# Decoder layer on one core: a quarter of the compression's page loads on GpSimd's queue, the loads' rooms in another order, two rings exchanged

## The chip, the cores and the metric

The kernel runs on one core of a Trainium2 chip. The metric is the device time of one execution in microseconds, as a median of runs. Engines are named as in the profile: PE (TensorE matmuls; PEld its weight loads), DVE (VectorE), ACT (ScalarE), POOL (GpSimd), SP (SyncE, which here only issues DMAs). A queue is the in-order list of instructions of one engine; what it issues as DMA moves later, on the 16 DMA engines.

## The reference

One decoder layer on 320 tokens (256 of a prompt, 64 of eight samples), width 2048: a first SwiGLU block with LayerNorm, a mixer (retention heads and sparse attention with a paged cache of 2048 past positions per sample), a second SwiGLU block. The change touches one part of the mixer, the compression of the cached keys and values of the eight samples:

```python
def compress(x, pos_emb, w1, w2):
    ...
    chunks = x[:, :n_chunks * CMP_STRIDE].astype(F32).reshape(B, n_chunks, CMP_STRIDE, NSA_KV_HEADS, NSA_HD)
    ...
    h = jnp.einsum('pd,pdf->f', pos_emb.astype(F32), w1f)
    for r in range(R):
        h = h + jnp.einsum('bnskd,sdf->bnkf', chunks, w1r[r])[:, r:r + n_cmp]
    return jnp.einsum('bnkf,fd->bnkd', jax.nn.gelu(h), w2.astype(F32))
```

It runs once on keys and once on values, over all pages of the cache that the page table names (8 samples x 16 pages of 128 positions).

## The kernel before, in words

All large products are made of three matmuls with a high and a low part of each factor (`mm3`, lines 211 to 216); `split` (lines 218 to 220) makes the two parts of a tile, the high one on ACT (L219), the low one on DVE (L220). One stream of emitted instructions sets the order on every engine; background tasks are woven in by a clock of estimates. [...]

The stage of interest, `compress` (L708 on), stands between the first SwiGLU block and the projection `w_in_nsa`. In the trace it runs from 946.9 us to 1279.0 us.

- **Work.** Eight pairs of samples (pairs 0 to 3 are keys, 4 to 7 values) of 16 steps n each, 128 steps in all. A step is 18 matmuls of 256 columns. m counts steps by twos (0 to 63). The data of a pair comes in two halves, 16 halves in all, each for four values of m.
- **Loads.** A half is 32 pages' tiles of 128 rows x 128 values, 64 KB each, one DMA per tile, since each page's address is read from the page table. `cx_load` calls `pages` for four tiles at a time; `pages` loads four addresses into registers of SP (L597) and issues four DMAs on SP's queue (L601). So SP issues 32 DMAs per half.
- **Rooms.** A half lies in one of three rooms of 16 KB per partition: `x0` and `x1`, cut from two rings which otherwise hold the layer's input parts, and `raw`, the weight buffers. The table `ROOMS` (L677) says which. A room is loaded anew when the half in it has been split. Half 0 and 1 come during the end of the first SwiGLU block (`down1_hook`); the table `loads` (L714 on) says at which m the others are issued. Half 3 is issued at m = 0 and 1, half 2 at m = 2 and 3.
- **Splits.** `cx_split(m + 2)` is emitted at step m: two sums on POOL (L702, tiles `t`), one split of 1024 columns and two of 256 on ACT and DVE. It needs the whole half.
- **Other work in the stage.** After each pair, `cpost` (L803) runs a gelu on DVE and ACT (its last DVE instruction is L801) and two products on PE (L208), and writes its result with a DMA on POOL's queue (L844). At n = 49 to 73 the weights of keys give way to those of values: eight times a DMA on SP (`K<-cw1v`, `cw_load`), a split (`cw_split`), a sum on POOL (L660) and another split (`cs_split`). At n = 112 `x_back` starts to load the layer's input back from DRAM (L790), `x_scale` (n = 117) and `x_parts` make its parts for `w_in_nsa`.

Of the kernel before, what the change touches and what calls it, by code (L numbers as in the profile page):

```python
# [9 lines left out]
F32R = mybir.dt.float32r  # L10
# [7 lines left out]
NT = 320  # L18
# [149 lines left out]
class Builder:  # L168
# [151 lines left out]
    def start(self):  # L320

        self.x_rings = [self.sb.ring(4 * KT * NT, name=f"x{k}") for k in range(2)]
        self.xh, self.xl = ([self.x_room(k, [128, NT], F32R) for _ in range(KT)] for k in range(2))
        raw = [self.t([128, 6, NT], f"G{5 + i}") for i in range(3)]
        self.xraw = [raw[q // 3][:, 2 * (q % 3):2 * (q % 3) + 2] for q in range(8)]
        for q in range(8):
            self.nc.sync.dma_start(out=self.xraw[q], in_=self.I["xT"][:, 2 * q:2 * q + 2, :])
            if q < 4:
                self.w_load()
        for q in range(2):  # L330
            self.x_split(q)
            self.w_split()
# [88 lines left out]
    def ln_residual(self, coef):  # L421
        nc = self.nc
        for m in range(KT):
            t1 = self.t([128, NT], "t", bufs=NTMP)
            nc.scalar.activation(t1, self.xl[m].bitcast(F32), AF.Copy, scale=coef)
            d = self.x_room(1, [128, NT])
# [113 lines left out]
    def ln_tiles(self, col):  # L540

        y = {}
        for step in range(KT + 2):
            if step < KT:
                self.ln_center(step, self.nc.gpsimd)
            m = step - 1
# [3 lines left out]
            m = step - 2  # L550
            if m >= 0:
                self.xl[m] = self.x_room(1, [128, NT], F32R)
                self.ln_split(m, col, y.pop(m))
# [40 lines left out]
    def pages(self, outs, name, b, j, part=slice(None)):  # L594

        a = b * 16 + j
        _, at = self.nc.values_load_multi_w_load_instructions(  # L597
            self.pts[0:1, a:a + len(outs)], engines=(mybir.EngineType.SP,), min_val=0, max_val=159,
            skip_runtime_bounds_check_because="a page table holds pages of the pool")
        for out, v in zip(outs, at):  # L600
            self.nc.sync.dma_start(out=out, in_=self.I[name][bass.ds(v, 1)].rearrange("o p f -> (o p) f")[:, part])  # L601
# [60 lines left out]
    def sums_room(self, i):  # L662
        return self.sums[:, 512 * i:512 * i + 512] if i < 4 else self.work[:, 512 * (i % 2):512 * (i % 2) + 512]

    def cs_split(self, i, r):

        if i < 6 and self.cs[i] is None:
            t = self.t([128, 2, 512], ("wh0", "wl0", "wh1", "wl1", "wh2", "wl2")[i], F32R)
            self.cs[i] = (t[:, 0], t[:, 1])
# [7 lines left out]
    ROOMS = "x0 raw x0 x1 x0 raw x1 x0 raw x1 x0 raw x1 x0 raw x1".split()  # L677

    def cx_load(self, half, first, last):
# [3 lines left out]
        for j in range(first, last, 4):  # L683
            outs = [room[:, 128 * k:128 * k + 128] for k in range(j, j + 4)]
            b = 2 * (pair % 4) + j // 16
            self.pages(outs, ("pkc", "pvc")[pair // 4], b, j % 16, slice(128 * h, 128 * h + 128))
# [23 lines left out]
    def compress(self):  # L710

        raw = {}

        loads = {}  # L714
        for half, first, n in ((3, 0, 16), (2, 2, 16), (5, 6, 8), (4, 10, 16)) + tuple((h, 4 * h - 10, 8) for h in range(6, 16)):
            for k in range(32 // n):
                loads.setdefault(first + k, []).append((half, n * k, n * k + n))
        for n in range(128):
# [57 lines left out]
            if n == 112:  # L776
                self.x_back(range(0, 12, 2))
# [8 lines left out]
    def x_back(self, tiles, room=None):  # L786

        for m in tiles:
            d = self.x_room(0, [128, 2, NT]) if room is None else room
# [13 lines left out]
    def cpost(self, pair, acc):  # L803
# [3 lines left out]
        work = self.work if pair < 7 else self.t([128, 1024], "r0")  # L807
# [906 lines left out]
    def x_parts(self):  # L1714

        for m in range(KT):
            yield lambda: self.x_normal > m and self.x_came and (self.compressed if m > 11 else self.rows_split)
            self.xh[m], self.xl[m] = (self.x_room(k, [128, NT], F32R) for k in range(2))
# [4 lines left out]
    def down1_hook(self, c):  # L1723
# [10 lines left out]
        if c == 0:  # L1734
            self.rooms = {"x0": self.x_room(0, [128, 4096]), "raw": self.raw.rearrange("p k f -> p (k f)")}
            self.work = self.x_room(0, [128, 1024])
# [16 lines left out]
    def rr_rest(self):  # L1753
# [9 lines left out]
        last = self.x_room(1, [128, 1024], F32R)  # L1763
        self.cs[6:8] = (k0[:, 1024:1536], k0[:, 1536:2048]), (last[:, 0:512], last[:, 512:1024])
# [104 lines left out]
```

## Time and profile before

| | |
|---|---|
| median of 3 runs | 2882.04 us (2879.98 to 2884.12) |
| profiled execution, its own time | 2881.62 us |
| its span in the trace | 2879.9 us |
| PE busy in the span | 2787.8 us (97%) |
| DVE, ACT, POOL busy | 1565.9, 1209.9, 409.0 us |
| the compression stage | 946.9 to 1279.0 us |

Read the table as follows. Some 1.7 us of the profiled time lie outside the span. A busy PE is not PE at its peak: matmuls overlap in the records, and at the lower of the clock's two levels they take twice as long and still count as busy. In a stretch of the trace the number of matmuls says more than the busy time. SP's issuing is not counted as busy in the profile; it is seen in the timeline of SP's queue.

### The profile page before, as it was taken

To read this page: it belongs to the slowest core of one execution; us is meant where nothing else is said; L and a number is where in the kernel's file an instruction comes from. 1 tells how busy PE (TensorE), PEld (TensorE's weight loads), DVE (VectorE), ACT (ScalarE), POOL (GpSimd) and SP (SyncE) were. 2 spreads that over 40 slices of the span, in tenths; PEclk is the share of its full clock that TensorE was granted. 3 is DMA by queue.
4 is the path that set the end of the run, shared out by engine and by line. 5 is a ranking of instruction groups with operands and counts; after the bars stand their busy time and mean duration, and the time that the engine had idled before them with its cause. 6 is when DMAs were issued, how large, how long until landed. Compare 5 with 4: busy or idle time off the path is not lost. (4 is left out here: it accounts for less than half of the span.)

```text
span 2879.9 us, 49773 instructions
## 1 busy us (share of the span) xinstructions
PE 2787.8 (97%) x19841; PEld 2710.1 (94%) x19841; DVE 1565.9 (54%) x1939; ACT 1209.9 (42%) x1748; POOL 409.0 (14%) x436
## 2 busy tenths in 40 slices
PE   9999999999999898999999999999999999999996
PEld 9999999999999887998888888989999999999996
DVE  4333333357768668784574455673333333367665
ACT  4333333344445445544443445343333333355453
POOL 0000000000103435433232111350000000001111
PEclk9999999999999999999999999999999999999998
DMA  6555444456657345347677764544444444444442
GB/s 225 180 193 179 151 148 153 148 161 200 198 166 236 109 124 147 110 158 243 194 234 247 231 216 164 199 131 154 153 147 153 147 151 149 150 147 149 147 150 92
DMA packets 215146, 484.76 MB, mean 168 GB/s; under 512 B 24257, under 2 KB 115266, under 8 KB 212994
## 3 DMA queue, kind: packets, MB, share of 16 engines
q1 hardware_dynamic: 208674, 458.64, 49.9%
q0 software_dynamic: 6240, 22.94, 2.2%
q8 instruction: 155, 2.54, 0.4%
q14 instruction: 77, 0.63, 0.1%
HBM read 467.47 MB, written 22.28 MB: 170 GB/s over the span
## 5 line engine op out<-in xcount | busy, mean ns | idle before, releaser
L220 DVE TENSOR_TENSOR wl<-raw,wh 128x1024 fp32r<-128x1024 f32 x650 | 814.0, 1253 | 1070.7 <-ACT wh L219 1045.5
L219 ACT ACTIVATE wh<-raw 128x1024 fp32r<-128x1024 f32 x650 | 688.1, 1059 | 1162.1 <-PE m L214 1122.2
L213 PE MATMUL m<-x,wh 128*128 128x320 f32 x3664 | 1145.6, 313 | 9.0 <-ACT wh L219 6.4
L214 PE MATMUL m<-x,wh 128*128 128x320 f32 x3664 | 1129.5, 308 | 3.4 <-DVE x L538 3.4
L215 PE MATMUL m<-x,wl 128*128 128x320 f32 x3664 | 1129.4, 308 | 0.4 <-DVE wl L220 0.4
L213 PEld LDWEIGHTS m<-x,wh 128*128 128x128 f32 x3664 | 689.1, 188 | 32.7 <-issue 22.8
L214 PEld LDWEIGHTS m<-x,wh 128*128 128x128 f32 x3664 | 689.2, 188 | 5.0 <-DVE x L538 4.2
L215 PEld LDWEIGHTS m<-x,wl 128*128 128x128 f32 x3664 | 688.6, 188 | 0.8 <-DVE wl L220 0.8
L213 PE MATMUL m<-r,wh 128*128 128x320 f32 (+1 forms) x1592 | 495.5, 311 | 2.2 <-ACT wh L219 1.0
L215 PE MATMUL m<-r,wl 128*128 128x320 f32 (+1 forms) x1592 | 490.8, 308 | 0.0
L214 PE MATMUL m<-r,wh 128*128 128x320 f32 (+1 forms) x1592 | 487.8, 306 | 2.8 <-DVE r L220 2.8
L213 PEld LDWEIGHTS m<-r,wh 128*128 128x128 f32 x1592 | 298.9, 188 | 8.1 <-issue 4.9
L214 PEld LDWEIGHTS m<-r,wh 128*128 128x128 f32 x1592 | 299.5, 188 | 4.8 <-DVE r L220 3.9
L215 PEld LDWEIGHTS m<-r,wl 128*128 128x128 f32 x1592 | 298.2, 187 | 0.0
L474 POOL TENSOR_TENSOR t<-x,x 128x320 f32<-128x320 f32 x3 | 2.7, 914 | 1415.1 <-DVE x L454 719.2
L220 DVE TENSOR_TENSOR r<-G,r 128x640 fp32r<-128x640 f32 (+1 forms) x184 | 157.1, 858 | 0.0
L213 PE MATMUL x<-r,G 128*128 128x256 f32 x480 | 139.4, 290 | 11.7 <-ACT r L219 11.7
L214 PE MATMUL x<-r,G 128*128 128x256 f32 x480 | 137.2, 286 | 2.0 <-DVE r L220 2.0
L215 PE MATMUL x<-r,G 128*128 128x256 f32 x480 | 136.2, 284 | 0.0
L219 ACT ACTIVATE r<-G 128x640 fp32r<-128x640 f32 (+1 forms) x184 | 130.1, 712 | 0.0
L213 PEld LDWEIGHTS x<-r,G 128*128 128x128 f32 x480 | 92.7, 193 | 13.5 <-ACT r L219 12.1
L702 POOL TENSOR_TENSOR t<-x 128x256 f32<-128x256 f32 x88 | 84.1, 979 | 101.6 <-DMA x<-pkc 45.2
(385 smaller groups left out, 2329.5 us busy)
## 6 DMA issues: line engine op xcount, KB each, us to landing
raw<-wup SPq DMA_DIRECT2D x352, 512.0 KB
raw<-wdn SPq DMA_DIRECT2D x176, 512.0 KB
raw<-win_ret SPq DMA_DIRECT2D x48, 512.0 KB
raw<-win_nsa SPq DMA_DIRECT2D x40, 512.0 KB
raw<-wout SPq DMA_DIRECT2D x32, 512.0 KB
x<-pkc SPq DMA_DIRECT2D x192, 64.0 KB
r<-pks SPq DMA_DIRECT2D x96, 128.0 KB
x<-pvc SPq DMA_DIRECT2D x160, 64.0 KB
```

Of the source, the lines that this page charges most:

```text
L213: mm(out, wh, xh, start=start, stop=False)
L214: mm(out, wh, xl, start=False, stop=False)
L215: mm(out, wl, xh, start=False, stop=stop)
L219: self.nc.scalar.activation(hi, src, AF.Copy)
L220: self.nc.vector.tensor_tensor(lo, src, hi.bitcast(F32), op=ALU.subtract)
L474: nc.gpsimd.tensor_tensor(s, self.d[0], self.d[1], op=ALU.add)
L702: self.nc.gpsimd.tensor_tensor(t.rearrange("p (g c) -> p g c", c=8), rows[:, s, 0], rows[:, s, 1], op=ALU.add)
```

## The change

Three things. `pages` can give the last `other` tiles of a call to POOL's queue; `cx_load` calls it for eight tiles at a time, six on SP and two on POOL, for halves 2 to 15 (halves 0 and 1 stay on SP). The rooms of the halves come in another order, and half 2 is now issued at m = 0 and 1, ahead of half 3 (m = 2 to 5). The rings swap roles: the last half lies in `x0`, the input that comes back goes to ring 1 with the high parts (`kh`), the low parts to ring 0 (`kl`); `work`, the space of `cpost`, gets a part of its own in each ring. The diff, nearly whole:

```diff
+        self.kh, self.kl = 0, 1
...
-            d = self.x_room(1, [128, NT])
+            d = self.x_room(self.kl, [128, NT])
...
-                self.xl[m] = self.x_room(1, [128, NT], F32R)
+                self.xl[m] = self.x_room(self.kl, [128, NT], F32R)
...
-    def pages(self, outs, name, b, j, part=slice(None)):
-
-        a = b * 16 + j
-        _, at = self.nc.values_load_multi_w_load_instructions(
-            self.pts[0:1, a:a + len(outs)], engines=(mybir.EngineType.SP,), min_val=0, max_val=159,
-            skip_runtime_bounds_check_because="a page table holds pages of the pool")
-        for out, v in zip(outs, at):
-            self.nc.sync.dma_start(out=out, in_=self.I[name][bass.ds(v, 1)].rearrange("o p f -> (o p) f")[:, part])
+    def pages(self, outs, name, b, j, part=slice(None), other=0):
+
+
+        cut = len(outs) - other
+        for queue, engine, k, n in ((self.nc.sync, mybir.EngineType.SP, 0, cut),
+                                    (self.nc.gpsimd, mybir.EngineType.Pool, cut, len(outs))):
+            if k == n:
+                continue
+            a = b * 16 + j
+            _, at = self.nc.values_load_multi_w_load_instructions(
+                self.pts[0:1, a + k:a + n], engines=(engine,), min_val=0, max_val=159,
+                skip_runtime_bounds_check_because="a page table holds pages of the pool")
+            for out, v in zip(outs[k:n], at):
+                queue.dma_start(out=out, in_=self.I[name][bass.ds(v, 1)].rearrange("o p f -> (o p) f")[:, part])
...
-        return self.sums[:, 512 * i:512 * i + 512] if i < 4 else self.work[:, 512 * (i % 2):512 * (i % 2) + 512]
+        return self.sums[:, 512 * i:512 * i + 512] if i < 4 else self.work[i // 6][:, 512 * (i % 2):512 * (i % 2) + 512]
...
+        if i == 7 and self.cs[i] is None:
+
+            t = self.x_room(0, [128, 2, 512], F32R)
+            self.cs[i] = (t[:, 0], t[:, 1])
...
-    ROOMS = "x0 raw x0 x1 x0 raw x1 x0 raw x1 x0 raw x1 x0 raw x1".split()
+    ROOMS = "x0 raw x1 x0 x1 raw x0 x1 raw x0 x1 raw x0 x1 raw x0".split()
...
-        for j in range(first, last, 4):
-            outs = [room[:, 128 * k:128 * k + 128] for k in range(j, j + 4)]
+        for j in range(first, last, 8):
+            outs = [room[:, 128 * k:128 * k + 128] for k in range(j, min(j + 8, last))]
...
-            self.pages(outs, ("pkc", "pvc")[pair // 4], b, j % 16, slice(128 * h, 128 * h + 128))
+            self.pages(outs, ("pkc", "pvc")[pair // 4], b, j % 16, slice(128 * h, 128 * h + 128), 2 if half > 1 else 0)
...
-        for half, first, n in ((3, 0, 16), (2, 2, 16), (5, 6, 8), (4, 10, 16)) + tuple((h, 4 * h - 10, 8) for h in range(6, 16)):
+        for half, first, n in ((2, 0, 16), (3, 2, 8), (5, 6, 8), (4, 10, 16)) + tuple((h, 4 * h - 10, 8) for h in range(6, 16)):
...
+                self.kh, self.kl = 1, 0
                 self.x_back(range(0, 12, 2))
...
-            d = self.x_room(0, [128, 2, NT]) if room is None else room
+            d = self.x_room(self.kh, [128, 2, NT]) if room is None else room
...
-        work = self.work if pair < 7 else self.t([128, 1024], "r0")
+        work = self.work[1] if pair < 7 else self.t([128, 1024], "r0")
...
+        self.x_room(self.kl, [128, 256])
         for m in range(KT):
...
-            self.xh[m], self.xl[m] = (self.x_room(k, [128, NT], F32R) for k in range(2))
+            self.xh[m], self.xl[m] = (self.x_room(k, [128, NT], F32R) for k in (self.kh, self.kl))
...
+            self.work = [self.x_room(0, [128, 1024])]
             self.rooms = {"x0": self.x_room(0, [128, 4096]), "raw": self.raw.rearrange("p k f -> p (k f)")}
-            self.work = self.x_room(0, [128, 1024])
...
-        last = self.x_room(1, [128, 1024], F32R)
-        self.cs[6:8] = (k0[:, 1024:1536], k0[:, 1536:2048]), (last[:, 0:512], last[:, 512:1024])
+        self.work.append(self.x_room(1, [128, 1024]))
+        self.cs[6] = k0[:, 1024:1536], k0[:, 1536:2048]
```

How the lists of the engines move, at three places. In these rows ISA is an instruction on registers, TENSOR_LOAD reads page addresses; line numbers of the changed kernel are larger by 8 to 16.

The first place is SP's list early in the stage, where one half ends and the next begins. Before (room x1 is `x_875`, room x0 is `x_790`; the half that ends is half 3, the one that begins is half 2):

```order
L601 DMA x_875_8868<-pkc 128x128
L601 ISA
L601 DMA x_875_8868<-pkc 128x128
L601 ISA
L601 DMA x_875_8868<-pkc 128x128
L601 ISA
L601 DMA x_875_8868<-pkc 128x128
L597 TENSOR_LOAD pts_376
L601 ISA
L601 DMA x_790_7885<-pkc 128x128
```

Now (room x0 is `x_791`; half 2 ends in x1, half 3 begins in x0):

```order
L609 DMA x_875_8864<-pkc 128x128
L609 ISA
L609 DMA x_875_8864<-pkc 128x128
L609 ISA
L609 DMA x_875_8864<-pkc 128x128
L609 ISA
L609 DMA x_875_8864<-pkc 128x128
L609 ISA
L609 DMA x_875_8864<-pkc 128x128
L605 TENSOR_LOAD pts_376
L609 ISA
L609 DMA x_791_7886<-pkc 128x128
```

A load of addresses serves six DMAs in place of four (one more of the six stands above the piece shown), and half 2 comes first.

The second place is POOL's list at the same time (`t` are the sums of `cx_split`, here for m = 2, 3 and on). Before:

```order
L702 TENSOR_TENSOR t_8872<-x_790_7885 128x256
L702 TENSOR_TENSOR t_8985<-x_790_7885 128x256
L702 TENSOR_TENSOR t_8987<-x_790_7885 128x256
L702 TENSOR_TENSOR t_9086<-raw_63 128x256
L702 TENSOR_TENSOR t_9088<-raw_63 128x256
```

Now:

```order
L714 TENSOR_TENSOR t_8868<-x_791_7886 128x256
L605 TENSOR_LOAD pts_376
L609 ISA
L609 DMA x_875_8864<-pkc 128x128
L609 ISA
L609 DMA x_875_8864<-pkc 128x128
L605 TENSOR_LOAD pts_376
L609 ISA
L609 DMA x_875_8864<-pkc 128x128
L609 ISA
L609 DMA x_875_8864<-pkc 128x128
L714 TENSOR_TENSOR t_8981<-x_791_7886 128x256
```

Four DMAs with two loads of addresses stand between the sums of one split and the next, at m = 0 and again at m = 1 and at m = 10 and 11; at the other m of the loads it is two DMAs and one load.

The third place is SP's list at the end of half 15 and the first loads of `x_back`, with the semaphores each waits for (DMAHW: a DMA issued by SP, DMASW: one issued by POOL). Before:

```order
L601 DMA x_875_8868<-pvc 128x128 [waits DMAHW6_49]
L790 DMA x_1028_13206<-x_aside 128x640 [waits DMAHW7_49,DVE_49,Pool_49]
L790 DMA x_1029_13208<-x_aside 128x640 [waits DMAHW0_49]
L790 DMA x_1030_13210<-x_aside 128x640 [waits DMAHW1_49]
L790 DMA x_1031_13212<-x_aside 128x640 [waits DMAHW2_49]
```

Now:

```order
L609 DMA x_791_7886<-pvc 128x128 [waits DMAHW6_49]
L804 DMA x_1029_13203<-x_aside 128x640 [waits DMASW4_49,DMASW3_49,DMASW5_49,DMASW2_49,DMASW6_49,DMASW1_49,DMASW7_49,DMASW0_49,DMAHW7_49,DVE_49,Pool_49]
L804 DMA x_1030_13205<-x_aside 128x640 [waits DMAHW0_49]
L804 DMA x_1031_13207<-x_aside 128x640 [waits DMAHW1_49]
L804 DMA x_1032_13209<-x_aside 128x640 [waits DMAHW2_49]
```

Half 15 is loaded to x0 instead of x1, and the first `x_back` load, now into x1, also waits for DMAs that POOL issued.

## Rows read from the trace of the kernel before

**Rows 1.** Table of stretches: length, busy per engine (instructions), clock, DMA share, GB/s.

```profile
932.00:947.00 15.00, 15.00 (x96) 14.13 (x94) 10.17 (x14) 6.93 (x12) 2.73 (x3) 1.00 0.49 137
947.00:982.00 35.00, 35.00 (x289) 34.28 (x288) 25.40 (x30) 18.31 (x34) 13.90 (x14) 1.00 0.39 114
982.00:998.00 16.00, 4.99 (x27) 4.49 (x26) 4.71 (x4) 4.82 (x8) 5.74 (x6) 0.68 0.37 106
998.00:1028.00 30.00, 29.15 (x239) 28.02 (x239) 21.67 (x33) 13.30 (x26) 10.27 (x11) 1.00 0.36 103
1028.00:1040.00 12.00, 9.25 (x65) 8.84 (x64) 3.99 (x5) 4.30 (x7) 4.88 (x6) 0.86 0.45 131
1040.00:1060.00 20.00, 18.39 (x151) 17.73 (x150) 18.12 (x26) 12.50 (x25) 12.35 (x14) 1.00 0.42 123
...
1088.00:1116.00 28.00, 20.91 (x152) 19.02 (x151) 20.99 (x28) 14.99 (x26) 13.78 (x13) 0.88 0.53 155
...
1132.00:1148.00 16.00, 8.87 (x53) 7.48 (x53) 13.22 (x19) 7.87 (x15) 6.99 (x7) 0.79 0.45 133
1148.00:1248.00 100.00, 100.00 (x852) 99.52 (x852) 76.90 (x101) 54.67 (x101) 42.22 (x49) 1.00 0.41 116
1248.00:1264.00 16.00, 14.49 (x125) 14.31 (x124) 15.84 (x20) 7.55 (x14) 12.86 (x12) 1.00 0.68 247
1264.00:1278.00 14.00, 10.16 (x67) 9.95 (x67) 9.11 (x17) 3.50 (x6) 2.26 (x3) 0.76 0.27 84
sum 346.00, PE 310.21 PEld 301.29 DVE 255.56 ACT 173.54 POOL 146.51; mean PE 23.86 PEld 23.18 DVE 19.66 ACT 13.35 POOL 11.27
```

**Rows 2.** Timeline of PE at the end of its first wait [idle before <-releaser].

```profile
993.31 0.58 PE L213 MATMUL x<-r,G 128*128 128x256 f32 x1 [10.09 <-ACT r L219]
```

**Rows 3.** Timeline of POOL at two waits for pages and a sum of the weights.

```profile
1033.34 1.41 POOL L702 TENSOR_TENSOR t<-x 128x256 f32<-128x256 f32 x2 [19.23 <-DMA x<-pkc]
...
1080.98 2.21 POOL L660 TENSOR_TENSOR K<-K 128x512 f32<-128x512 f32 x1 [4.58 <-DVE G L220]
...
1245.40 3.99 POOL L702 TENSOR_TENSOR t<-x 128x256 f32<-128x256 f32 x4 [8.82 <-DMA x<-pvc]
```

**Rows 4.** Timeline of SP's queue: start, length, line, what was issued.

```profile
899.03 1.96 SPq L601 DMA_DIRECT2D x<-pkc  x4
...
950.44 40.05 SPq L601 DMA_DIRECT2D x<-pkc  x64
...
1011.96 35.34 SPq L601 DMA_DIRECT2D x<-pkc  x56
...
1222.58 21.05 SPq L601 DMA_DIRECT2D x<-pvc  x32
1243.74 2.74 SPq L790 DMA_DIRECT2D x<-x_aside  x6
```

**Rows 5.** Waits of SP's queue, 940 to 1245 us: total, times, longest.

```profile
SPq L448 <- DVE r L220: 0.4, 1, 0.4
SPq L601 <- POOL t L702: 0.2, 1, 0.2
```

**Rows 6.** Instructions of SP's queue by line: duration ns min/median/max.

```profile
L601 SPq DMA_DIRECT2D x<-pkc x192: 332/333/1373, 899.0 to 1073.2; - x192
...
L597 SPq TENSOR_LOAD <-pts x160: 293/300/561, 898.3 to 1675.5; - x160
...
L269 SPq DMA_DIRECT2D raw<-wup x352: 327/328/1187, 1.2 to 2517.8; - x176
```

**Rows 7.** DMAs that POOL issues, by line and in its timeline.

```profile
L844 POOL DMA_DIRECT2D c_aside<-x x7: 557/557/780, 1036.5 to 1272.3; - x7
...
1315.52 2.65 POOL L925 DMA_DIRECT2D kvo<-G  x5 [0.29 <-POOL G L922]
...
1496.61 0.95 POOL L1124 DMA_INDIRECT r<-pvs,vrow  x1 [0.30 <-issue]
1497.86 0.94 POOL L1124 DMA_INDIRECT r<-pvs,vrow  x1 [0.30 <-issue]
```

**Rows 8.** POOL's sums by group, 947 to 1278 us: busy, mean ns.

```profile
L702 POOL TENSOR_TENSOR t<-x 128x256 f32<-128x256 f32 x84 | 79.9, 975 | 79.7 <-DMA x<-pkc 45.2 <-DVE r L220 13.8 <-DMA x<-pvc 11.5
L702 POOL TENSOR_TENSOR t<-raw 128x256 f32<-128x256 f32 x40 | 33.3, 852 | 22.9 <-DVE r L220 10.2 <-DMA raw<-pvc 8.0 <-DVE K L220 4.2
L660 POOL TENSOR_TENSOR K<-K 128x512 f32<-128x512 f32 x8 | 14.7, 1834 | 35.1 <-DVE G L220 35.1
```

**Rows 9.** PE's waits between 1040 and 1280 us: total, times, longest.

```profile
PE m L208 <- DVE x L801: 21.2, 6, 7.1
```

**Rows 10.** Timeline of ACT, and of SP before it, at a weight load.

```profile
1095.07 0.38 SPq L647 DMA_DIRECT2D K<-cw1v  x1
...
1098.88 1.06 ACT L219 ACTIVATE G<-K 128x1024 fp32r<-128x1024 f32 x1 [2.30 <-DMA K<-cw1v]
```

## The prediction

> **What bounds the kernel now.** PE is busy for 97% of the span, so the first question is where the rest is. I read the table of stretches first [rows 1]. The count of matmuls tells more than the busy time: from 1148 to 1248 us PE runs without a gap at full clock and does 852 matmuls in 100 us, 0.1174 us each, the products of `cpost` included. That is the undisturbed pace, 16.9 us for the 144 matmuls of a half. A stretch's loss is its length less its count times 0.1174 us; this takes in idle time and the time at the lower clock (the granted clock falls to 0.68 to 0.88 as a mean of stretches with a wait, so part of each ran at 1.2 GHz). A few matmul records may be missing, which could make losses look larger by a few us in all.
>
> - **A**, 982 to 998: 27 matmuls, loss 12.8 us.
> - **B**, 998 to 1060: 1.9, 4.4 and 2.3, together 8.6 us.
> - **C**, around the exchange of weights, 1088 to 1116 and 1132 to 1148: 10.2 and 9.8, together 19.9 us.
> - **D**, 1248 to 1278: 1.3 and 6.1, together 7.5 us.
>
> The stage lasts 332.1 us, of which 48.8 are lost: about 283 would be left.
>
> Next is who is late. In A, PE waits 10.09 us for a split [rows 2]; in B, POOL's sums wait 19.23 us for pages, and before D again 8.82 us [rows 3]. The pages come from SP's queue [rows 4], and there the reader should see that it is full: 64 pages in 40.05 us, and the stretches follow on each other from 950 to 1243.6. In 940 to 1245 SP waits for anything for 0.6 us in all [rows 5]. It is bound by issuing: 20.0 us for a half of 32 pages, against 16.9 us that PE needs. The DMA engines are not the limit: at 0.36 to 0.45 of their time they carry 103 to 133 GB/s, and 247 GB/s in a stretch at 0.68 [rows 1].
>
> **The change, part by part.**
>
> *SP's load.* A batch of four takes 40.05/16 = 2.50 us. One alone takes 1.96 us from the first issue to the last's end, with 0.333 us for an issue [rows 4, 6], so issues follow on each other by (1.96 - 0.33)/3 = 0.54 us, and 0.34 us are left for the addresses (a TENSOR_LOAD has 0.30) [rows 6]. A batch of six then takes 0.34 + 6 x 0.54 = 3.6 us, and a half with four such batches 14.3 in place of 20.0 us. Over 14 halves SP gives up 79 us. With 14.3 below 16.9, SP no longer bounds the stage; from half 6 on a load waits for its room instead, for which it has about four m (16 us) to spare until its split.
>
> *POOL's load.* 14 x 8 = 112 DMAs come to POOL, with 56 loads of addresses. No POOL DMA in the trace takes its address from a register. The nearest rows: plain ones take 0.557 us as a median, or 2.65/5 = 0.53 in a row; indirect ones, which read 128 offsets, follow on each other by 1.25 us [rows 7]. On SP a register in the address made no difference, 0.333 against 0.328 us [rows 6]. So I take the plain row plus SP's surcharges, 0.15 for half a load of addresses and 0.12 for the registers: 0.83 us, with 0.53 and 1.25 as ends (a plain issue that took 0.78 beside a busy DVE is inside). That is 93 us. POOL is now busy for 146.5 - 2.7 = 143.8 us of the stage [rows 1]; with 93 it is 237 us of some 305, 78%. Per half it is 8 x 0.83 + 8 sums of 0.91 [rows 8] = 13.9 us, below 16.9. In the exchange of weights eight sums of 1.84 us over 3.1 halves add 4.7: 18.7 us per half there.
>
> *Behind POOL's waits.* The first DMA to a room waits until DVE has read the half before; behind it stand the sums of the next split, which need tiles `t` that DVE gives back at nearly the same time. Splits run two m, 8 us, ahead of PE, so I cost this at nothing outside C; if that cover is gone, each half pays the wait once.
>
> *Half 2 first, in x1.* SP's share is issued from 950.4 to 964.8. POOL has to issue 16 DMAs and make 12 sums and two sums of weights (2.2 each) before half 2's first split: 951 + 13.3 + 10.9 + 4.4 = 979.6, ACT and DVE end some 2 us later, and PE needs it at 982.4 plus 1.4 (its third group of matmuls). So A goes with 2 us to spare; at 1.25 us an issue 5 us of it stay. I leave 1.5: gain **11.3** of 12.8.
>
> *Half 4.* Four halves are issued by 950.4 + 57.4 = 1007.8; PE comes to half 4 two halves after 982.4, at 1016. Before, its last page was issued near 1032 [rows 4]. B should go but for the first `cpost` waits: gain **7.0** of 8.6.
>
> *The exchange of weights.* C is another wait: PE stands at products of `cpost` behind the gelu's last DVE instruction, 21.2 us in six waits of 1040 to 1280 us [rows 9]. DVE is busy 21.0 of 28 and 13.2 of 16 us there [rows 1]; its gaps come from the chain DVE, POOL sum, ACT, DVE (POOL's sum waited 4.58 us for DVE) [rows 3]. SP's part of it: a weight load issued at 1095.07 stood behind pages, though POOL's sum out of its place had ended at 1083.2 [rows 3, 10], and ACT waited 2.30 us for it [rows 10]. That goes. In exchange 24 or so DMAs come between POOL's sums in this chain. Below, nothing excludes a loss: eight sums, each later by one issue of 0.83, make -6.6. Above, POOL's 18.7 us per half leaves (18.7 - 16.9) x 3.1 = 5.6 of the 19.9, a gain of 14.3. Nearest is the one wait the rows show: gain **3.0**.
>
> *The end.* `x_back` was issued at 1243.74, right behind half 15 [rows 4], and DVE is busy 15.84 of 16 us after 1248 [rows 1], making up what came late. With both early the work lies under PE's last steps: gain **6.0** of 7.5. The swapped rings give `x_back` a room, x1, whose half 13 is long split; that costs nothing, and without it the load would wait for half 15's splits. Its added wait for POOL's DMAs is for pages long landed.
>
> *The rest.* Batches of eight for half 1 save SP 1.3 us where nobody waits. `work` and `cs[7]` in other places and the 256 columns left free are addresses alone. After the stage the lists are the same, and PE's next work starts earlier by the gain.
>
> Sum: 11.3 + 7.0 + 3.0 + 6.0 = 27.3 us. The profiled execution has 2881.62 us, 0.4 below the median of 2882.04; forecast **2854.3 us**, stage about 305 us.
>
> **A rule against it.** The rows say that the issue is the limit [rows 4, 5]. The Trainium skill, page "DMA: Bandwidth & Descriptors", section "Issuing engines are not separate DMA queues", says that DMAs started from several engines run on the same 16 DMA engines, and that this saves only the sequencer's time, "usually small relative to the DMA itself". By that rule the sum would be zero; here the sequencer's time is the larger, as the share of 0.36 to 0.45 shows [rows 1].
>
> **The rivals.**
>
> *C eats part (chance 0.16).* POOL's issues lengthen the chain in the exchange: -6.6 instead of +3.0, and A keeps 5. That is 27.3 - 9.6 - 3.5 = 14 us: 2867. For it: DVE and POOL hand work to each other there. Against: a split lead of 8 us.
>
> *All losses go (0.08).* C gains 14.3: 38.6 us or a little more, 2842. Against it: DVE's share of 0.8.
>
> *POOL becomes the bound (0.10, the other side).* POOL's list is in order, and each split's sums stand behind its DMAs. If an issue takes more than (332.1 - 143.8)/112 = 1.68 us, POOL alone needs longer than the stage now does, and each 0.1 us above costs 11.2 us; at 1.85 it is 351 us, so 2901. For it: a register address on POOL was never seen, and a plain issue rose from 0.557 to 0.780 once [rows 7]. Against: both ends of the price lie below 1.68. The Trainium skill, page "SBUF — State Buffer", section "SBUF: two separate sides", has a mechanism for it: descriptors for GpSimd's DMAs can't be written while DVE runs an instruction in a two-port mode, its example going from about 620 to about 3100 ns. By 3.1 us an issue the stage would be an estimated 491 us; the page excepts two-input tensor instructions, which nearly all of DVE's here are.
>
> *Nothing moves (0.04).* If the DMA engines and not SP's issuing set 0.62 us a page, a second queue brings nothing: 2881.6. The stretch with 247 GB/s speaks against it [rows 1].
>
> **How the numbers follow.** The forecast has 0.62; its own range is 2844 (C gains 13) to 2864 (C loses 6.6). With the first rival's 2867 and what lies behind it, and part of the second, 2838 to 2874 leaves out POOL as the bound, no movement and a little of the tail of the second. A measurement of this kernel can tell about 0.2%, 5.8 us. Faster by more: 0.62 + 0.16 + 0.08 = 0.86; same 0.04; slower 0.10.
>
> **What would show it.** Right: SP's queue in the stage has waits for rooms, of tens of us in all; PE's idle gap near 982 is gone; POOL's DMAs take 0.6 to 1.2 us and POOL has 220 to 260 us in the stage; losses are left at 1060 to 1130 behind L801's successor. Wrong: POOL without idle time through the stage, or splits that wait for sums on POOL at every half; or SP still without a wait.

## The result and the profile after

The changed kernel takes **2865.39 us** (median of 5 runs, 2860.59 to 2869.96), the kernel before 2882.04: a ratio of 0.9944, with an interval of 0.9929 to 0.9959. It is faster by 16.7 us, where 27.3 were forecast; the range held, the forecast is 11 us too low. The profiled execution has 2862.96 us and a span of 2861.3, 18.6 less than before.

The table of stretches of the changed kernel, with the edges of [rows 1]:

```profile
982.00:998.00 16.00, 16.00 (x139) 16.00 (x138) 15.43 (x18) 8.84 (x17) 13.53 (x20) 1.00 0.48 137
998.00:1028.00 30.00, 29.58 (x241) 28.24 (x240) 18.34 (x25) 13.01 (x25) 13.86 (x23) 1.00 0.44 126
1028.00:1040.00 12.00, 7.46 (x64) 7.25 (x62) 11.55 (x16) 6.71 (x13) 9.52 (x15) 0.99 0.57 169
1040.00:1060.00 20.00, 19.88 (x146) 18.40 (x147) 11.92 (x19) 9.82 (x17) 7.78 (x13) 0.92 0.50 143
...
1116.00:1132.00 16.00, 8.16 (x50) 6.74 (x49) 13.88 (x15) 9.79 (x17) 10.85 (x13) 0.79 0.45 133
...
1148.00:1248.00 100.00, 100.00 (x856) 100.00 (x855) 81.69 (x104) 53.32 (x99) 65.00 (x85) 1.00 0.45 138
```

A is gone: 139 matmuls in 982 to 998 instead of 27. B isn't: 64 in 1028 to 1040 leave 4.5 us lost there. In the exchange a stretch at the granted clock of 0.79 is left, only earlier. Since everything moves by 13 us after A, fixed edges compare different work from there on. A fixed point in the work is better: the first copy that `cpost` makes of each pair, on ACT. For pair 1 it is this row of ACT's timeline, before and after:

```profile
1041.81 0.37 ACT L815 ACTIVATE x<-x 128x256 f32<-128x256 f32 x1
```

```profile
1026.60 0.37 ACT L829 ACTIVATE x<-x 128x256 f32<-128x256 f32 x1
```

From such rows comes the table that the rest of this text uses, for all kernels. The first column is the start of pair 0's copy, the next three are distances between copies, the fifth is the start of pair 7's, all in us. An undisturbed pair takes 35.5 to 35.7 (pairs 4 to 6, in nearly all kernels). P0 shows A, P0 to P2 shows B, P2 to P4 the exchange C, P4 to P7 shows D.

| kernel | P0 | P0 to P2 | P2 to P4 | P4 to P7 | P7 | median |
|---|---|---|---|---|---|---|
| before | 999.1 | 76.6 | 89.4 | 125.5 | 1290.7 | 2882.04 |
| changed | 986.2 | 78.0 | 89.6 | 122.1 | 1275.9 | 2865.39 |
| e1_order_only | 983.4 | 90.2 | 89.4 | 123.3 | 1286.3 | 2877.19 |
| e2_pool_only | 991.7 | 70.9 | 89.8 | 122.9 | 1275.4 | 2863.64 |
| e3_other3_first | 986.9 | 69.9 | 89.6 | 122.4 | 1268.8 | 2862.20 |
| e4_cpost_late | 986.1 | 75.9 | 93.7 | 121.9 | 1277.6 | 2873.37 |
| e5_no_pool_exchange | 986.3 | 78.4 | 87.7 | 122.6 | 1275.0 | 2864.62 |
| e7_four_three_one | 986.0 | 87.6 | 89.6 | 122.0 | 1285.2 | 2873.20 |
| e8_no_low_of_values | 985.0 | 78.7 | 79.2 | 122.5 | 1265.3 | 2855.07 |
| e9_half_on_pool | 989.9 | 70.7 | 90.5 | 123.0 | 1274.1 | 2861.19 |
| f1_loads_of_four | 985.9 | 73.2 | 89.6 | 122.5 | 1271.2 | 2857.40 |
| f2_lows_on_pool | 985.2 | 74.9 | 91.3 | 122.6 | 1274.0 | 2862.67 |
| f3_combined | 990.4 | 71.2 | 91.4 | 122.2 | 1275.2 | 2864.07 |
| f4_sum_elsewhere | 985.6 | 73.0 | 86.9 | 122.4 | 1267.8 | 2853.55 |

At P7 the changed kernel is ahead by 14.8 us: 12.9 from A, -1.4 from B, -0.2 from C, 3.4 from D. The other 3.8 us of the profiled pair arise behind the stage. They are not put down to the change: behind P7 all kernels have nearly the same lists, yet the profiled executions take between 1583 and 1594 us there, and a product's wait for a DMA alone from 0.6 to 3.2 us. So single microseconds are compared up to P7 only, and medians that lie 3 or 4 us apart are not told apart. The steadiest distance is P2 to P4: it is 89.4 to 89.8 us in seven of the fourteen kernels.

SP's queue after, where [rows 4] stood before:

```profile
951.96 31.04 SPq L609 DMA_DIRECT2D x<-pkc  x48
...
984.04 15.86 SPq L609 DMA_DIRECT2D raw<-pkc  x24
...
1000.94 28.74 SPq L609 DMA_DIRECT2D x<-pkc  x42
...
1194.87 16.29 SPq L609 DMA_DIRECT2D x<-pvc  x24
...
1212.55 2.71 SPq L804 DMA_DIRECT2D x<-x_aside  x6
```

A half takes 15.5 to 16.4 us on SP instead of 20.0, but not 14.3. Half 4 is the first 24 of the 42; counted in the trace, the last of its pages is issued at 1016.1, where 1007.8 was forecast. What is longer is the load of addresses; instructions of the two queues by line, against [rows 6]:

```profile
L605 SPq TENSOR_LOAD <-pts x100: 297/716/1253, 898.9 to 1659.6; - x100
L605 POOLq TENSOR_LOAD <-pts x56: 503/508/995, 950.5 to 1204.5; - x56
```

0.716 us as a median on SP in place of 0.300. Sixteen loads in four halves make 16 x 0.42 = 6.7 of the 8.3 us by which half 4 is late. Timelines of POOL, DVE and PE show what follows from it:

```profile
1018.60 1.43 POOL L714 TENSOR_TENSOR t<-x 128x256 f32<-128x256 f32 x2 [15.36 <-DMA x<-pkc]
...
1019.63 1.48 DVE L220 TENSOR_TENSOR r<-x,r 128x1024 fp32r<-128x1024 f32 x1 [9.32 <-DMA x<-pkc]
...
1038.78 1.20 DVE L815 SCALAR_TENSOR_TENSOR x<-x 128x512 f32<-128x512 f32 x1
...
1040.12 2.05 PE L208 MATMUL m<-x,cw2k 128*128 128x512 f32 x2 [4.66 <-DVE x L815]
```

POOL waits 15.36 us for half 4 and DVE 9.32; DVE then works until 1042 us, idle for less than 1 us, on the splits that came late, the gelu's last instruction stands in its list behind them, and PE waits for that. The wait of [rows 2] has become one of the kind of [rows 9]. PE's waits of 940 to 1290 us:

```profile
PE m L208 <- DVE x L815: 21.2, 6, 7.8
PE x L214 <- DVE r L220: 1.3, 2, 1.0
```

And SP's queue now has waits (940 to 1245 us, the first rows; before, [rows 5]). L609 are the pages, which wait for rooms; L655 (`cw_load`) and L269 wait for the places of weights. So SP isn't the bound of the whole stage any more:

```profile
SPq L269 <- DVE r L220: 14.5, 1, 14.5
SPq L269 <- DVE x L831: 10.0, 1, 10.0
SPq L655 <- DVE x L810: 9.5, 2, 6.7
SPq L655 <- DVE wl L220: 9.5, 3, 3.3
SPq L609 <- DVE r L220: 5.7, 2, 5.4
```

### The profile page after: what moved, and what is told of

It is laid out like the page before. It is cut to its first block, busy times and chain, and to the rows that moved or that the text cites. A ratio compares the mean times of both kernels' runs of the same rounds, so it can differ in the third digit from the quotient of the medians.

```text
span 2861.3 us, 49912 instructions
## 1 busy us (share of the span) xinstructions
PE 2786.0 (97%) x19841; PEld 2708.4 (95%) x19841; DVE 1580.3 (55%) x1939; ACT 1210.4 (42%) x1748; POOL 464.9 (16%) x548
## 5 line engine op out<-in xcount | busy, mean ns | idle before, releaser
L214 PEld LDWEIGHTS x<-r,G 128*128 128x128 f32 x480 | 91.4, 190 | 3.4 <-DVE r L220 2.0
L213 PEld LDWEIGHTS x<-r,G 128*128 128x128 f32 x480 | 91.9, 192 | 1.4 <-issue 1.2
```

What stands on the lines that cost most here:

```text
L213: mm(out, wh, xh, start=start, stop=False)
L214: mm(out, wh, xl, start=False, stop=False)
```

## The experiments

Twelve kernels were run, each beside the kernel before. Diffs are against the changed kernel, unless another is named.

**Order and rooms alone.** All pages on SP, the rest as changed.

```diff
-..., 2 if half > 1 else 0)
+..., 0)
```

> The changed kernel with all pages on SP's queue again, in batches of eight; rooms, order of the halves and rings as changed. Theory 1 (SP's issuing bounds the stage, and the order alone only moves the wait): half 2 is in by about 972 us, so the wait near 982 goes, but half 4's last page is issued near 1034 as before, so PE or DVE waits there longer, and the last half is issued near 1243 again; time 2874 to 2886 us, no more than 8 us faster than the kernel before. Rival (the order is what brought the gain, since it removes the longest wait of PE): 2864 to 2870 us.

2877.19 us, ratio 0.9985 (0.9976 to 0.9994). A is gone here too (P0 at 983.4): half 2 comes first. But the same lateness comes back one pair later, P0 to P2 90.2 us, as one wait of PE:

```profile
1032.21 0.58 PE L213 MATMUL x<-r,G 128*128 128x256 f32 x1 [13.90 <-ACT r L219]
```

So the order moves the wait from half 2 to a later half, and brings about 4 us.

**POOL's queue alone.** Rooms, order and rings as before, batches of eight with two on POOL. The edit is the change without its lines on `ROOMS`, `loads`, `kh`, `kl`, `work` and `cs[7]`.

> The kernel before, with its rooms, its order of halves and its rings, but batches of eight with two of them on POOL's queue for halves 2 to 15. Theory 1: what counts is SP's pace of about 15.5 us a half; half 2, issued second, is in by 983 to 985 us, so PE waits there some 2 to 5 us, half 4 comes when it does in the changed kernel, and the time is 2863 to 2872 us. Rival (the order brought the gain): the wait near 982 stays at 8 us or more and the time is 2874 us or more.

2863.64 us, ratio 0.9935 (0.9922 to 0.9949), no more than the changed kernel takes. So the gain is that of the queue. The order's part is small beside it: A keeps 5.5 us of its loss (P0 at 991.7), but B loses 7.1 less.

**More of the early pages on POOL**, to bring half 4 sooner without touching its splits.

```diff
-..., 2 if half > 1 else 0)
+..., (3 if half < 6 else 2) if half > 1 else 0)
```

> The changed kernel with three of eight pages on POOL for halves 2 to 5 (two for the others). Theory 1 (SP is still the bound up to half 4, whose lateness leaves DVE idle for 9.3 us near 1010 and comes back as a wait of PE for DVE's gelu near 1036): half 4 is in by about 1008 us, DVE's idle time there falls below 3 us, the loss of some 6.5 us at 1032 to 1046 falls to 2 or less, and the time is 4 to 6 us below the changed kernel's, 2859 to 2862 us. Rival (the wait for the gelu at 1036 is DVE's own load and has nothing to do with the pages): the loss there stays at 5 to 8 us and the time is within 2 us of the changed kernel's 2865.

2862.20 us, ratio 0.9923 (0.9908 to 0.9937). SP begins half 4 at 993.59 instead of 1000.94:

```profile
993.59 29.52 SPq L609 DMA_DIRECT2D x<-pkc  x38
```

B is gone: P0 to P2 takes 69.9 us, no longer than two undisturbed pairs (71). This shows the cause of B, the late half 4. P7 is 7.1 us earlier than in the changed kernel, while the median is 3 us lower; in the two profiled executions, 6.4 of the 7.1 us come back behind P7.

**The gelu's product later in PE's list**, so that PE would have other work while the gelu ends.

```diff
-            yield 2.5
+            yield 6.0
```

> The changed kernel with the two products of cpost emitted 6.0 us of the emission clock after the gelu's last DVE instruction instead of 2.5. Theory 2 (PE's six waits of 21.2 us for the gelu are a matter of where the products stand in PE's list; DVE as a whole keeps up): the waits fall to 8 us or less and, with the clock's share, the time falls by 10 to 18 us, to 2848 to 2856 us. Rival (DVE's load in the exchange of weights is the bound; PE waits for a split instead of for the gelu): the waits move to the splits, time 2860 to 2868 us.

2873.37 us, ratio 0.9967 (0.9955 to 0.9979), above what either theory gave. This kernel changes part of the computation: the samples' output, which takes the compressed keys and values, is another. PE's waits of 940 to 1290 us:

```profile
PE m L208 <- ACT x L829: 8.6, 3, 6.0
PE x L214 <- DVE r L220: 7.3, 7, 1.6
PE m L213 <- ACT x L539: 7.1, 1, 7.1
PE m L208 <- DVE x L815: 3.0, 2, 2.6
```

The wait for the gelu falls from 21.2 to 3.0 us and others take its place, for the splits and for the next copies out of the accumulators; P2 to P4 gets longer. The place of the product isn't what holds PE.

**No pages on POOL during the exchange.**

```diff
-..., 2 if half > 1 else 0)
+..., 2 if half > 1 and half not in (8, 9, 10, 11) else 0)
```

> Halves 8 to 11 have all pages on SP again; the rest is as in the changed kernel. Theory A (POOL's issues lengthen the chain DVE, POOL sum, ACT, DVE in the exchange of weights): the loss at 1060 to 1148 us falls from about 19 to 12 us or less, the time to 2856 to 2860. Theory B (the exchange is set by DVE's own load, POOL's issues lie in its gaps): the loss there stays within 3 us, the time within 2863 to 2868. Theory C (SP needs the help there too): a half without POOL takes SP 20 us or more, so the four halves cost 16 us of lead; with no more than that in hand the split of half 10 or 11 waits for pages, the loss there grows and the time is 2868 to 2878.

2864.62 us, ratio 0.9943 (0.9930 to 0.9957); P2 to P4 87.7 us against 89.6. POOL is busy for 45.7 us of 1060 to 1148 instead of 60.0, and the exchange takes 1.9 us less; with no pages on POOL at all, in the run with the order alone, it takes 89.4. So POOL's issues cost at most 1.9 us of it, where the rival that C eats part had them cost 9.6 (-6.6 instead of +3.0). That rival falls, though its 2867 is close to what was measured.

**Batches of four, three on SP and one on POOL.**

```diff
-        for j in range(first, last, 8):
-            outs = [... for k in range(j, min(j + 8, last))]
+        for j in range(first, last, 4):
+            outs = [... for k in range(j, min(j + 4, last))]
...
-..., 2 if half > 1 else 0)
+..., 1 if half > 1 else 0)
```

> Batches of four pages, three on SP and one on POOL, in place of eight, six and two. The share of POOL is the same, the number of address loads doubles, each for half as many addresses. Theory A (a load of addresses has a price per address: 0.30 us for four, 0.72 for six): with three it takes 0.30 us or less, a half on SP takes 8 x (0.25 + 3 x 0.54) = 15 us as now or 1 us less, and the time is 2862 to 2867. Theory B (the rise to 0.72 comes from POOL, which loads addresses from the same row at the same time): SP's loads stay at 0.5 us or more, a half takes 8 x (0.7 + 1.62) = 18.5 us, SP bounds the first halves again and the time is 2869 to 2877. POOL has 112 loads of one address in place of 56 of two: at 0.5 us each, 28 us more on POOL under either.

2873.20 us, ratio 0.9976 (0.9967 to 0.9985). The loads of addresses, by queue:

```profile
L605 SPq TENSOR_LOAD <-pts x160: 294/669/1422, 898.1 to 1668.7; - x160
L605 POOLq TENSOR_LOAD <-pts x112: 281/287/666, 949.9 to 1215.3; - x112
```

Three addresses take 0.669 us, more than twice what four took [rows 6]. A half takes some 18 to 19 us on SP, and P0 to P2 is 87.6. The time is where theory B put it, but its reason can't be right: in the next run but one, half of the pages on POOL, SP's 64 loads of four addresses take 0.303 us as a median while POOL loads addresses from the same table.

**The low parts of the value weights left out.** The edit keeps ACT's instruction of `split` and drops DVE's, for both splits of the exchange.

> The low parts (DVE) of the value weights' splits during the exchange, eight of 1024 and eight of 512 columns, are left out: the products with them use the key weights' low parts. PE, ACT, POOL and SP have the same lists. Theory A (DVE's load in the exchange is what holds the gelu of cpost, and so PE): the loss at 1060 to 1148 us falls from about 19 to 8 us or less and the time to 2850 to 2857. Theory B (the gelu is late by the latencies between DVE and ACT in cpost, with DVE free in between): the loss stays above 14 us and the time at 2860 to 2867.

2855.07 us, ratio 0.9907 (0.9894 to 0.9921); P2 to P4 79.2 us, 10.4 less. The rows of 1060 to 1148 us, first of the changed kernel, then of this one:

```profile
1060.00:1148.00 88.00, 73.64 (x574) 69.64 (x573) 76.90 (x88) 49.02 (x86) 59.97 (x73) 0.94 0.45 134
```

```profile
1060.00:1148.00 88.00, 82.08 (x662) 79.25 (x661) 69.41 (x82) 54.16 (x96) 65.96 (x86) 0.96 0.50 150
```

At 0.1174 us a matmul the loss falls from 20.6 to 10.3 us. So DVE's part in the exchange is what holds PE for half of that loss, as theory A said (it asked for a little more, a loss of 8). Whether by its length or by its place in a chain this run can't say, as it takes away both.

**Half of the pages on POOL.**

```diff
-..., 2 if half > 1 else 0)
+..., 4 if half > 1 else 0)
```

> Half of the pages on POOL in place of a quarter: 224 DMAs, 112 more. It measures the rival that POOL becomes the bound. At 0.68 us a page, as the changed kernel's trace has it, POOL needs 16 x 0.68 + 8 x 0.91 = 18.2 us for a half, 23 in the exchange, against 16.9 of PE. Theory A (the price holds and POOL's list bounds the stage): the stage is some 14 x 1.3 + 5 us above the undisturbed pace, POOL has idle time under 10% of it, SP waits, and the time is 2868 to 2890. Theory B (the lead of the splits covers it): 2858 to 2868. Were the price to rise with POOL's share, to 1 us or more, the time would pass 2900.

2861.19 us, ratio 0.9932 (0.9917 to 0.9947): theory B. POOL issues 224 DMAs and is not the bound; SP waits 74.1 us for rooms.

```profile
SPq L609 <- DVE r L220: 74.1, 9, 13.1
```

B is gone (70.7), while P0 is 3.6 us later, as POOL has 32 pages to issue before half 2's first split.

**Loads of addresses by fours.** The times of all loads so far were 0.287, 0.508, 0.67, 0.30, 0.53, 0.72 and 0.52 us for 1, 2, 3, 4, 5, 6 and 8 addresses. This kernel gives POOL the last four of sixteen pages, so that every list has four or eight.

```diff
-..., 2 if half > 1 else 0)
+..., 4 if half > 1 and j // 8 % 2 else 0)
```

> The same quarter of the pages is on POOL, as the last four of every sixteen instead of the last two of every eight, so each list of addresses has four or eight entries, never six or two. The loads of addresses in the runs so far took 0.29, 0.51, 0.67 (SP) or 0.73 (POOL), 0.30 to 0.33, 0.53, 0.72 and 0.52 us for 1, 2, 3, 4, 5, 6 and 8 addresses. Theory A (four neighbouring addresses are read in one step, what is left over in a step each): SP's loads take 0.30 and 0.52, a half takes SP 2 x (0.82 + 12 x 0.54) = 14.6 us instead of 15.6, POOL's loads 0.32; half 4 is issued 3 to 4 us earlier, DVE's idle time near 1010 us falls from 9.3 to 6 us or less and the loss at 1032 to 1046 from 6.5 to 4 us or less; the time is 2859 to 2863 if nothing is given back, 2863 to 2866 if the exchange takes it. Theory B (the 0.72 came from another cause than the number): half still 15.5, time 2863 to 2868.

**2857.40 us**, ratio 0.9915 (0.9902 to 0.9929): 8 us below the changed kernel with the same share on POOL, and below the 2859 to 2863 that theory A gave. The loads of 947 to 1215 us, and the places where DVE and PE waited:

```profile
L605 SPq TENSOR_LOAD <-pts x56: 299/516/971, 950.9 to 1202.8; - x56
L605 POOLq TENSOR_LOAD <-pts x28: 314/322/575, 950.9 to 1199.5; - x28
```

```profile
1015.34 1.49 DVE L220 TENSOR_TENSOR r<-x,r 128x1024 fp32r<-128x1024 f32 x1 [5.30 <-ACT r L219]
...
1036.38 1.10 PE L208 MATMUL m<-x,cw2k 128*128 128x512 f32 x2 [1.82 <-DVE x L815]
```

A half takes 14.6 us on SP (29.19 for the first two), DVE's wait falls from 9.32 to 5.30 us and PE's from 4.66 to 1.82; P0 to P2 is 4.8 us shorter. The loads take the times that theory A gave, so its rule fits all that were seen: four neighbouring addresses cost one step, what is left over a step each. P7 is 4.7 us earlier, the medians are 8.0 apart; what is between lies within the spread of the runs.

**Low parts on POOL.** As the last, but halves 8 to 11 all on SP, and DVE's 256-column low parts of m = 26 to 39 on POOL.

> Loads of four as in the run before, no pages on POOL for halves 8 to 11, and the low parts of the two small splits (256 columns) of the steps m = 26 to 39 on POOL instead of DVE: 28 instructions of 0.79 us off DVE, on POOL some 28 of 1.0 us, against 32 DMAs of 0.65 us that POOL gives up. Theory A (DVE's load is the bound in the exchange): DVE loses 22 us there, nearly the 25 us of the run without the values' low parts; the loss at 1060 to 1148 us falls from 18 to 10 us or less and the time to 2851 to 2858. Theory B (POOL is now the slow hand: each small split waits for a POOL that also has the sums of the weights): POOL's list is the one waited for, PE waits for a split, and the time is 2862 to 2872.

2862.67 us, ratio 0.9933 (0.9921 to 0.9945), P2 to P4 91.3 us. The rows of 1060 to 1148, first of the run before, then of this one:

```profile
1060.00:1148.00 88.00, 74.20 (x572) 70.41 (x571) 75.49 (x87) 49.36 (x83) 58.18 (x74) 0.92 0.43 131
```

```profile
1060.00:1148.00 88.00, 74.39 (x561) 70.71 (x560) 58.61 (x58) 49.35 (x84) 71.79 (x70) 0.90 0.44 131
```

The timelines of DVE and of POOL at PE's longest wait:

```profile
1117.58 1.74 DVE L220 TENSOR_TENSOR G<-K,G 128x1024 fp32r<-128x1024 f32 x1
...
1124.16 1.22 DVE L220 TENSOR_TENSOR K<-K,K 128x512 fp32r<-128x512 f32 x1 [3.18 <-ACT K L219]
1125.30 0.68 DVE L815 SCALAR_TENSOR_TENSOR x<-x 128x512 f32<-128x512 f32 x1
```

```profile
1119.86 2.38 POOL L220 TENSOR_TENSOR r<-t,r 128x256 fp32r<-128x256 f32 x2
1122.21 1.25 POOL L668 TENSOR_TENSOR K<-K 128x512 f32<-128x512 f32 x1
```

DVE is busy for 58.6 us instead of 75.5, POOL for 71.8 instead of 58.2, and PE does no more. DVE stands idle for 3.18 us before the low part of a weight's sum, and the gelu's last instruction is behind that in its list. This low part stands at the end of a round trip: DVE makes the low part of the weight, POOL may only then write the sum into the weight's own place, ACT makes the sum's high part, DVE its low part. Here DVE's first part is done at 1119.3, but POOL makes the sum only from 1122.21 on, behind two of the low parts that this run gave it. That is theory B, and the time is in its range. The run doesn't test DVE's load alone, since the work went to another engine of the same round trip.

**The same with half of the early pages on POOL** (four of eight for halves 2 to 5).

> As the run before, with half of the pages of halves 2 to 5 on POOL (four of eight). If term B is only the late half 4, and DVE's load the only bound of the exchange, the loss at 1032 to 1046 us goes too (below 2 us, from 6.5) and the time is 2846 to 2853; if what is won before 1060 is given back in the exchange, as with three of eight on POOL, 2851 to 2858.

2864.07 us, ratio 0.9942 (0.9929 to 0.9955), above its expectation: P0 is 4 to 5 us later, as with half of the pages on POOL before, and P2 to P4 is as in the last run.

**The round trip cut.** Against the kernel with loads of four: POOL's sum goes to two small tiles ahead of the weight's split.

```diff
-                self.cw_split(k, raw[k])
+                halves = [self.t([128, NT], "t", bufs=NTMP)[:, 0:256] for s in range(2)]
+                for s, t in enumerate(halves):
+                    self.nc.gpsimd.tensor_tensor(t, raw[k][:, 512 * s:512 * s + 256], raw[k][:, 512 * s + 256:512 * s + 512], op=ALU.add)
+                self.cw_split(k, raw.pop(k))
...
-                r = raw.pop(k)
-                place = r.rearrange("p (s h f) -> p s h f", s=2, h=2)[:, :, 0]
-                self.cw_sum(place, r)
-                self.cs_split(k, place)
+                for s, t in enumerate(halves):
+                    self.split(*(a[:, 256 * s:256 * s + 256] for a in self.cs[k]), t)
```

> On the kernel with loads of four: POOL's sum of a value weight goes to two small tiles, ahead of that weight's split, instead of into the weight's own place behind it. Busy time of DVE, ACT and POOL stays about the same; what goes is POOL's wait for DVE's low part of the weight (23.3 us in seven waits of 1030 to 1150 us), and with it the way DVE, POOL, ACT, DVE on which the next low part, and the gelu's last instruction behind it in DVE's list, stand. Theory A (this round trip, not DVE's load, holds the gelu): the loss at 1060 to 1148 us falls from about 18 to 10 us or less, the time from 2857.4 to 2845 to 2852. Theory B (DVE's load holds it): the loss stays at 15 us or more, the time 2854 to 2860. Theory C (the two more small tiles of five make the sums of the splits wait): POOL waits for DVE at those tiles instead, 2858 to 2870.

**2853.55 us** (2851.61 to 2856.43), ratio 0.9897 (0.9879 to 0.9915), the lowest median of all: none of its runs is as slow as the fastest of the changed kernel (2860.59). POOL's waits of 1030 to 1150 us in the kernel with loads of four, then here:

```profile
POOL K L668 <- DVE G L220: 23.3, 7, 5.2
POOL c_aside L858 <- ACT x L852: 15.9, 3, 9.4
```

```profile
POOL c_aside L859 <- ACT x L853: 15.0, 2, 9.5
POOL t L714 <- DVE r L220: 13.2, 10, 3.2
```

Its row of 1060 to 1148 us:

```profile
1060.00:1148.00 88.00, 76.66 (x595) 72.87 (x594) 80.86 (x97) 51.47 (x94) 64.31 (x86) 0.92 0.46 138
```

The wait for the weight's low part is gone. P2 to P4 is 2.7 us shorter, which is clear of how far this distance varies otherwise. The median is 3.9 lower, which is not: the intervals of the two ratios overlap. Both are less than theory A asked for, and 595 matmuls leave a loss of 18.1 us, as in theory B. DVE is now busy for 80.9 of 88 us, and at PE's longest wait, which ends at 1120.60, the gelu's last instruction comes at 1119.77, behind DVE's work of 1107.97 on, with no gap above 0.2 us. With the loads of four alone DVE had no such gap before that instruction either, from 1111.28 to 1122.68. So DVE's list is full there with the round trip or without it. Cutting the round trip alone brought 2.7 us of P2 to P4; the run without the low parts, which has less for DVE to do and no wait of POOL for them, brought 10.4. What a shorter list on DVE alone would bring was not tried.

## Why the prediction came out as it did

- **What bounds the kernel: right.** SP's issuing was the limit. With a quarter of the pages elsewhere and nothing else the time falls to 2863.64. The Trainium skill, page "DMA: Bandwidth & Descriptors", section "Issuing engines are not separate DMA queues", calls the time that a second issuing engine saves "usually small relative to the DMA itself". This case is outside that "usually": a second queue alone brought some 17 us, with the DMA engines at a share of 0.36 to 0.45 before [rows 1].
- **A, 11.3 forecast: right.** 12.9 at P0.
- **B, 7.0 forecast, -1.4 measured: the step that failed.** It is the sentence "A batch of six then takes 0.34 + 6 x 0.54 = 3.6 us, and a half with four such batches 14.3": the load of addresses was carried over from four to six as if it had one price. It has 0.72 for six, half 4's last page is issued 8.3 us later than "by 1007.8", and with it DVE falls behind and PE waits for the gelu. The run with three of eight on POOL gets B back whole, the run with loads of four 4.8 us of it. This term is 8.4 of the 12.6 us that the four terms miss up to P7 (27.3 forecast, 14.7 measured).
- **C, 3.0 forecast, -0.2 measured: mis-sized.** The bounds held. The wait that was to go, ACT's 2.30 us for a weight behind pages, is not among ACT's waits any more, and nothing was gained by it. The prediction named the chain of DVE, POOL, ACT and DVE, and took its gain from a wait beside it. What the runs showed in its place is that P2 to P4 gets shorter by 10.4 us without DVE's low parts of the weights, by 2.7 with the round trip cut, and by no more than 1.9 without POOL's issues. How DVE's load and the round trip share the 10.4 stays open.
- **D, 6.0 forecast, 3.4 measured up to P7.** The input is issued at 1212.55 instead of 1243.74, as said. With the order alone it is issued at 1238.33, and P4 to P7 is 123.3 against 122.1 and, before, 125.5: 2.2 of the 3.4 us need no more than the first 5 us of those 31. With POOL's queue alone, the rings as before, it is issued at 1211.17 and P4 to P7 is 122.9, so the exchange of the rings shows no gain of its own. The rest of the 6.0 is a wait that the prediction had as gone: the work behind `x_back` does not lie under PE's last steps. PE's wait for the gelu's last DVE instruction, before and after (1240 to 1290 us, and its timeline), and a stretch of the changed kernel:

```profile
PE m L208 <- DVE x L801: 5.4, 2, 3.8
```

```profile
1254.57 1.86 PE L208 MATMUL m<-cw2v,x 128*128 128x128 f32 x8 [2.21 <-DVE x L815]
```

```profile
1252.00:1258.00 6.00, 3.79 (x21) 3.58 (x20) 4.98 (x10) 0.60 (x1) 0.61 (x2) 0.74 0.09 16
```

  21 matmuls in 6 us at a granted clock of 0.74 leave some 3.5 us lost. In front of that instruction DVE works from 1239.00 on almost without a gap, on the last splits and on the input's scaling.
- **POOL's price: 0.83 forecast, about 0.68.** An issue took 0.537 us as a median:

```profile
L609 POOL DMA_DIRECT2D x<-pkc x40: 537/537/772, 952.3 to 1043.8; - x40
```

  All 112 took 61.3 us, and POOL stood idle before them for 15.1 us in which it waited for nothing that the profile shows, loads of addresses included (timeline of POOL, 947 to 1262 us): 76.4/112 = 0.68. Two signs named for being right fail with this price: an issue is below 0.6 to 1.2 us, and POOL was busy for 198.95 us of that stretch, not for 220 to 260. With twice the pages on POOL the stage was no longer, so the rival of POOL as the bound was as unlikely as was said, and more. The Trainium skill, page "SBUF — State Buffer", section "SBUF: two separate sides", has GpSimd's descriptors wait while DVE runs an instruction in a two-port mode. Here no issue of POOL took more than 0.772 us, with DVE busy for 82% of the time; but nearly all that DVE runs here has two inputs, which the page excepts, so these runs don't test it.
- **The rivals.** The time lies nearest to the rival that C eats part (2867), and its mechanism is not what happened: C neither gained nor lost, and A kept nothing. That the sum came near it is chance.

## What to carry to other kernels

Price a queue by all that it issues, address loads included, and measure that price for the very number that the change uses; lists in multiples of four were the cheap ones here. When a wait goes, follow the next data that come late through each in-order list behind it: A's 12.9 us were real, and half 4, late by 8.3 us, took back what B was to give. And before work is moved off a busy engine, see where the other engine stands in the same chain: 17 us of DVE's work in the exchange went to POOL for nothing, since POOL's sum then came later, and the gelu behind it.

## What the runs showed of the hardware that was not expected

- A load of page addresses to registers costs by steps: 0.287, 0.508 and 0.669 us for one, two and three addresses, 0.300 for four, 0.528 for five, 0.716 for six, 0.525 for eight. All seven fit one step for each four neighbours and one for each left over, the first 0.3 us and each further one some 0.2. Whether it matters where in the table the four begin was not tried.
- DVE's small subtractions took longer in the runs in which POOL issues more DMAs. The same 42 instructions in 947 to 1262 us, with no pages on POOL (order alone), a quarter (changed) and a half:

```profile
L220 DVE TENSOR_TENSOR K<-t,K 128x256 fp32r<-128x256 f32 x42 | 20.0, 513 | 1.3 <-ACT K L219 1.3
```

```profile
L220 DVE TENSOR_TENSOR K<-t,K 128x256 fp32r<-128x256 f32 x42 | 27.5, 695 | 0.0
```

```profile
L220 DVE TENSOR_TENSOR K<-t,K 128x256 fp32r<-128x256 f32 x42 | 35.0, 869 | 1.3 <-ACT K L219 1.3
```

  A mean of 513, 695 and 869 ns, while the large ones from the same rooms (128x1024, 43 of them) have 1563, 1485 and 1511. So work moved to POOL's queue is not free for DVE, and the prediction had no term for it. The traces tell something of the cause, if all 126 subtractions of 256 columns in that stretch are sorted by what POOL does at the same time. In the changed kernel the 42 beside an idle POOL take 0.417 us as a mean, the 20 beside an issue alone 0.413, and the 64 beside one of POOL's sums 0.972: there the sums lengthen them and the issues don't. With half of the pages on POOL, 10 of the 33 beside an issue alone take some 0.95 us, and why these do is open.
